# One factor chain at the beginning, squares on two engines, an own tile for an exp, side stages in more visits, rope tables kept: a hybrid mLSTM and sliding-window decoder layer

## The chip, the cores and the metric

The kernel runs on one core of one Trainium2 chip. Its time is the device time of one execution in microseconds. The profile is a trace of one execution; times inside it are counted from its first instruction. Engines are named as the profile names them: PE (matmuls; PEld for its weight loads), DVE (vector), ACT (scalar), POOL (GpSimd), SP (the queue that issues all DMAs here).

## The reference

One layer over a prompt of 1024 rows and 8 samples of 4 rows, width 1024, all in f32. Cut to what matters:

```python
mod = silu(c) @ w_ada + b_ada;  shift, scale, gate = split(mod, 3)
h = rmsnorm(x, g_norm) * (1 + scale) + shift
mq, mk, mv, mi, mf, mo, mz, aq, ak, av, az, gm, ga = split_in(h @ w_in)
# mLSTM branch: 4 heads of 128, scanned in chunks of 128 rows
b = cumsum(logsigmoid(mf + b_f)); d = b[t] - b[s] + (mi + b_i)[s], causal
m_hat = max(b + m, max(d)); s = (q k^T) * exp(d - m_hat)
num = s v + exp(b + m - m_hat) * (q C);  dot = sum(s) + exp(b + m - m_hat) * (q n)
y_m = norm(num / max(|dot|, exp(-m_hat))) * g_mn * sigmoid(mo) * silu(mz)
# attention branch: 8 heads of 64, 2 kv heads, window 128, a sink per head
q, k = partial_rope(aq), partial_rope(ak)
y_a = softmax_with_sink(q k^T / 8, window) v * silu(az)
u = sigmoid(gm) * (y_m @ w_mo) + sigmoid(ga) * (y_a @ w_ao)
y = rmsnorm(x + gate * (u @ w_o), g_final)      # plus new states and caches
```

The samples go through the same layer with states and caches of their own.

## The kernel before, in words

Products are in split f32: an operand is a high part and a rest, and three matmuls (high x high, high x rest, rest x high) stand for one product. `h` lies in SBUF transposed (features on partitions, the 1056 rows on the free axis), as eight blocks k of 128 features, in tiles `h_h` and `h_l`.

**Beginning.** `load_x` issues the loads of x in parts of 512 rows (p = 0 and 1, eight tiles each) and `xS` for the samples (p = 2). `x_sq` (from L337) squares the tiles on ACT, and PE sums them over partitions into `xs`, copied to `xsum`. `x_rs` turns the sums into columns (`xc`), computes one over the root with a chain of small DVE operations (`recip_sqrt`: `ssq`, `xr_y`, `xr_w`), and puts each block's factors on a diagonal (`xdg`). `x_rows` spreads them to rows with matmuls (`xb`), and `x_mul` multiplies x by them on DVE. `ada_chunk` makes 512 columns of the scale or the shift (`ada_sc`, `ada_sh`, transposed as `adat_sc`, `adat_sh`), which end in the tiles `A` and `B`. `h_part` then applies `A` and `B` on ACT and splits into `h_h` and `h_l`; `h_samples` does it for the samples. `pair` issues the first products (`g_ak`, `g_av`), first for the k of `half[0]`, then for those of `half[1]`. In the factor chains (L1471 to L1477) part 0 has a chain of its own and parts 1 and 2 share one. While `V.on` and `S.on` hold (to L1506), DVE and ACT keep the order in which the code issues.

**Main part.** Jobs of the product with `w_in` follow: four groups of queries (`queries`), then `mq`, `mk`, `mv` of four heads (`head_jobs`), then the gates as blocks of a Strassen-like scheme (`block_products`, `bx`, `by`, `bz`, `bw`), then `att_out`, `mem_out` and the product with `w_o` (`fo`). PE's order is written out when the program is built. Beside the main products, `Side` steps generators: a generator issues some operations and yields a lag and the PSUM pools that its next visit needs; `side.now` counts modelled product time, and a generator is visited again when its lag is over, its pools aren't used in the same tick, and 2.0 have passed since the last visit with products. The generators are:

- `gates` (L515): the sums of the mLSTM gates, in steps. The tile `bTs` is stored to `m_s` and then overwritten by its exp (L636), which is transposed a visit later (L648). A row of sums is copied from PSUM as `row`.
- `unit(g, b0)` (L740): 16 units of attention, two blocks of 128 queries each: scores `sc`, masked maximum on DVE (`mx`, `nmx`), exps on ACT (`p`, `den`), division on DVE, transposes `pt`, product `oT`. From `sc` to the division all is issued in one visit, and the transposes 11.0 later.
- `head(h)` (L941): three groups of chunks a head, in stages a (transposes `tk`, `tv`, the exps of `et` with a mask added by POOL), b (`S`, `U`, states `C`), c (`n`, sums of squares, `factors`: 13 or more small DVE operations) and d (transposes `ty`).
- `sample_head(h)` (L1051): the same for the samples; a step makes the tiles `vm` from `vf` on DVE and ACT, and products `sU` and `st` follow.
- `sum_blocks`: sums of blocks of `h` for the gates' scheme.

DVE, ACT, POOL and SP execute in the order that a scheduler lays down when the program is built, from priorities and modelled times; each is a queue, and an instruction that waits holds up all behind it. Most SBUF tiles come from a pool `half` of 42 buffers, raw weights from one of 9, and PSUM tiles from four pools (g, a, b, o) of two banks each. `rope_load` loads the cosine and sine tables: six tiles for the keys in `attention_begin`, and six again in each of the four `queries(g)`. `rope` uses them: a shuffle and two operations on DVE, one on POOL.

Of the kernel before, what the change touches and what calls it, by code (L numbers as in the profile page):

```python
# [26 lines left out]
NH = 4  # L27
# [131 lines left out]
def body(tc, a):  # L159
    nc = tc.nc  # L160
    with ExitStack() as ctx:
# [104 lines left out]

        xT = [load_x(p) for p in range(2)]
        xS = ht([128, KT, NS], "xS")
        dma(xS, a["xS"])
        xT.append([xS[:, k] for k in range(KT)])  # L270

# [65 lines left out]
        def x_sq(p):  # L337
            n = PARTS[p][1]
            acc = po([128, 512], f"xs{p}")
            if p == 2:  # L340
                sqs = ht([128, KT, NS], "xsq2")
                S.activation(sqs, xS, AF.Square)
            for k in range(KT):
                if p == 2:
                    sq = sqs[:, k]
                else:
                    sq = ht([128, 512], "xsq")
                    S.activation(sq, xT[p][k], AF.Square)
                j = 32 * (k % 4)
                mm(acc[j:j + 32, :n], one[:, 0:32], sq, start=(k < 4), stop=(k >= 4), share=4)  # L350
            sums = ht([128, 512], "xsum")
            S.copy(sums[:, :n], acc[:, :n])
            return sums

        def x_rs(ps_, sums):
            blocks = [(p, i, min(128, PARTS[p][1])) for p in ps_ for i in range(-(-PARTS[p][1] // 128))]
            nb = len(blocks)
            cols = pg([128, nb], f"xc{ps_[0]}")
            for j, (p, i, m) in enumerate(blocks):
                mm(cols[:m, j:j + 1], sums[p][:, i * 128:i * 128 + m], cst[:, C_S9:C_S9 + 1], start=True, stop=True)  # L360
            ssq = cp.tile([128, nb], F32, name=f"ssq{nb}")
            if m < 128:
                V.memset(ssq[:, nb - 1:nb], 1.0)
                V.tensor_scalar(ssq[:m, nb - 1:nb], cols[:m, nb - 1:nb], 1.0 / D, EPS, op0=ALU.mult, op1=ALU.add)
            full = nb - (m < 128)
            V.tensor_scalar(ssq[:, :full], cols[:, :full], 1.0 / D, EPS, op0=ALU.mult, op1=ALU.add)
            rs = recip_sqrt(ssq, [128, nb], f"xr{nb}")
            dgs = {p: ht([128, 512], f"xdg{p}") for p in ps_}
            for j, (p, i, m) in enumerate(blocks):
                V.tensor_scalar(dgs[p][:m, i * 128:i * 128 + m], ident[:m, :m], rs[:m, j:j + 1], None, op0=ALU.mult)  # L370
            return dgs
# [143 lines left out]
        def gates(zg, bias):  # L515
# [119 lines left out]
            dma(a["m_s"], v3(bTs)[:, :, 3])  # L635
            S.activation(bTs, bTs, AF.Exp, scale=-1.0)  # L636
            mle = cp.tile([NH, NS], F32, name="mle")
# [9 lines left out]
            fq = pb([128, 128], "fq2")  # L647
            tr(fq[:NS, 0:4], bTs, ident[:NH, :NH])  # L648
            tr(fq[:NS, 4:8], mle, ident[:NH, :NH])
# [44 lines left out]
        def ev_ak(p, acc, c0, n):  # L694
            k = ht([128, 384], "kr")[:, :n]
            S.copy(k, acc[:, :n])
            at["kl"] = ht([128, 384], "krr")
            t = rope(k, at["rope"][p], n, at["kl"], kD, c0)
            if p == 2:
                V.tensor_tensor(at["kTs"], k[:, 256:288], t[:, 256:288], op=ALU.add)  # L700
                del at["rope"]

# [37 lines left out]
        def unit(g, b0):  # L740
# [25 lines left out]
            v2 = lambda t: t.rearrange("p (k i) -> p k i", i=2)  # L766
            V.tensor_tensor(v2(nmx[:, 4:8]), sink[:, :, g:g + 1].to_broadcast((128, 2, 2)), v2(mx), op=ALU.subtract)
            den = sm([128, 4], "den", 3)
            S.activation(nmx[:, 4:8], nmx[:, 4:8], AF.Exp)
            for kv in range(2):  # L770
                for i, lo in enumerate(los):
                    j = 2 * kv + i
                    S.activation(p[kv][:, i, lo:], p[kv][:, i, lo:], AF.Exp, bias=nmx[:, j:j + 1],
                                 accum_out=den[:, j:j + 1])
            V.tensor_tensor(den, den, nmx[:, 4:8], op=ALU.add)
            V.reciprocal(den, den)
            for kv in range(2):
                for i, lo in enumerate(los):
                    j = 2 * kv + i
                    V.tensor_scalar(p[kv][:, i, lo:], p[kv][:, i, lo:], den[:, j:j + 1], None, op0=ALU.mult)  # L780
            yield 11.0, "b"
            pT = [ht([128, 4, 128], f"pT{kv}") for kv in range(2)]
# [21 lines left out]
        def queries(g):  # L804
            cs = [rope_load(p) for p in range(3)]

# [134 lines left out]
        def head(h):  # L941
# [11 lines left out]
            def stage_a(p):  # L953
# [22 lines left out]
                G.tensor_tensor(et[:, :m], et[:, :m], cmask.unsqueeze(1).to_broadcast((128, m, 128)), op=ALU.add)  # L976
                for i in range(m):
                    S.activation(et[:, i], et[:, i], AF.Exp, bias=an[:, j0 + i:j0 + i + 1])
                qw = ht([128, 3, 128], "qw")
                dma(qw[:, :m], st["wid"][j0:j0 + m].unsqueeze(0).to_broadcast((128, m, 128)))  # L980
                G.tensor_tensor(qw[:, :m], qw[:, :m], q[:, :w].rearrange("p (c e) -> p c e", e=128), op=ALU.mult)
                w_[p] = q, k, kn, vn, vw, et, qw, ns

            def stage_b(p):
# [21 lines left out]
            def stage_c(p):  # L1006
# [10 lines left out]
                for i in range(m):  # L1017
                    jk = sm([128, 128], "mjk", 2, BF16)
                    S.activation(jk, ns[:, i, 0:128], AF.Square, accum_out=ssq[:, i:i + 1])
                f = factors(ns[:, :m, 128], fl[:, j0:j0 + m], ssq[:, :m], [128, m], f"f{m}")  # L1020
                for i in range(m):
# [14 lines left out]

            for visit in ([(load, 0), 10.0, "b"], [(stage_a, 0), 13.0, "o"], [(stage_b, 0), (load, 1), 10.0, "ob"],
                          [(stage_c, 0), (stage_a, 1), 13.0, "o"], [(stage_b, 1), (load, 2), 4.0, "b"], [(stage_d, 0), 6.0, "ob"],
                          [(stage_c, 1), (stage_a, 2), 13.0, "o"], [(stage_b, 2), 4.0, "b"], [(stage_d, 1), 6.0, "o"],
                          [(stage_c, 2), 15.0, "b"], [(stage_d, 2), 0.0, ""]):  # L1040
                for fn, p in visit[:-2]:
# [9 lines left out]
        def sample_head(h):  # L1051
# [21 lines left out]
            S.activation(et, et, AF.Exp, bias=an[:NS, 32 + h:33 + h])  # L1073
            V.tensor_tensor(et, et, S_[:NS], op=ALU.mult)
            qd = ht([128, 8, 36], "qd")
# [7 lines left out]
            for b, m in zip(bs, ns_):  # L1083
                vf, vm = ht([NS, 512], f"vf{h}"), ht([96, 512], f"vm{h}", F32R)
                w = m * 129 + m % 2
                if m % 2:
                    G.memset(vf[:, w - 1:w], 0.0)
                V.tensor_tensor(vf[:, :m * 129].rearrange("p (b e) -> p b e", e=129), vn.unsqueeze(1).to_broadcast((NS, m, 129)),
                                wm[:, b].unsqueeze(2).to_broadcast((NS, m, 129)), op=ALU.mult)
                S.copy(vm[0:32, :w], vf[:, :w])  # L1090
                V.tensor_tensor(vm[32:64, :w], vf[:, :w], vm[0:32, :w].bitcast(F32), op=ALU.subtract)
                V.tensor_copy(vm[64:96, :w], vf[:, :w])
                vms.append(vm)
            yield 9.0, "o"
            num = po([128, 129], f"sn{h}")
# [8 lines left out]
            for i, (c, b, m) in enumerate(zip(Cs, bs, ns_)):  # L1104
                up = pb([128, 388], f"sU{h}_{i}")
                mm(up[:, :m * 129 + m % 2], kn, vms[i][:, :m * 129 + m % 2], start=True, stop=True)
                V.tensor_tensor(c[:, :m], c[:, :m], up[:, :m * 129].rearrange("p (b e) -> p b e", e=129), op=ALU.add)
# [8 lines left out]
            jk = sm([128, 128], "mjk", 2, BF16)  # L1116
            S.activation(jk[:NS], ns[:, 0:128], AF.Square, accum_out=ssq)
            f = factors(ns[:, 128:129], fls[:, h:h + 1], ssq, [NS, 1], "fs")
            V.tensor_scalar(ns[:, 0:128], ns[:, 0:128], f, None, op0=ALU.mult)
            yield 13.0, "b"  # L1120
            ty = pb([128, NS], f"sty{h}")
# [71 lines left out]
        def sum_blocks():  # L1193
            for n in ("t2", "t3", "t4"):
                blocks[n] = []
            for k in range(4):
# [4 lines left out]
                G.tensor_tensor(b22, b22, b12, op=ALU.subtract)  # L1201
                G.tensor_tensor(b11, b11, b22, op=ALU.add)
                yield 2.0, ""
                block_split("t3", k, b22)
                yield 1.0, ""
                block_split("t2", k, b11)
# [263 lines left out]
        sh1 = ada_chunk(ada_load(1, "sh1", "l1"), "sh1", shift_done(1))  # L1470
        sums = {0: x_sq(0)}  # L1471
        dgs = x_rs((0,), sums)
        sums[1] = x_sq(1)
        rows = {0: x_rows(0, dgs[0])}
        sums[2] = x_sq(2)
        x_mul(0, rows[0], half[0])
        dgs.update(x_rs((1, 2), sums))  # L1477
        steps(sc0, 3)
        for p in (1, 2):
            rows[p] = x_rows(p, dgs[p])  # L1480
        run(sc0)
        x_mul(1, rows[1], half[0])
        x_mul(2, rows[2], None)
        run(sh0)
# [4 lines left out]
        for k in half[0]:  # L1489
            h_part(k, 0)  # L1490
            if k == 0:
                prefetch(order[1])
        pair(half[0], 0, acc[0])
        for k in half[0]:
            h_part(k, 1)
        steps(sc1, 3)
        pair(half[0], 1, acc[1])
        h_samples(half[0])
        x_mul(0, rows[0], half[1])
        x_mul(1, rows[1], half[1])  # L1500
# [293 lines left out]
```

## Time and profile before

| | us |
|---|---|
| median of three runs | 906.91 |
| the three runs | 906.37, 906.91, 910.14 |
| the profiled execution | 909.59 |
| its span, first to last instruction | 907.8 |

Mean granted PE clock of the profiled execution: 0.977 of full speed. DMA: 118,380 packets, 152 MB, 167 GB/s on average, but 309 GB/s in the first 20 us and 400 in the next 20.

The page gives the busy time of each engine, and the span in 40 slices. The table of waits says which engine stood still before which instruction, and whose result ended the wait. The timeline lists instructions in order of time with the idle time before each. A view of stretches gives busy times and the granted clock between two moments. An engine's idle time costs only where PE in the end waits for it, since PE is the busiest.

### The profile page before, as it was taken

How to read it: one execution, taken by the hardware profiler on the slowest of the kernel's cores; microseconds unless marked ns; L12 is line 12 of the kernel's file. 1: busy time of each engine (PE TensorE's matmuls, PEld its weight loads, DVE VectorE, ACT ScalarE, POOL GpSimd, SP SyncE). 2: the span in 40 equal slices, each digit the busy share in tenths (PEclk: the TensorE clock that was granted, in tenths of full speed). 3: DMA queues.
4: the chain of work that ended last, by engine and by line, in shares of the span. 5: the costliest groups of instructions: out<-in, count | busy, mean ns of one | idle time of the engine just before them, and what ended most of it. 6: DMA issues, size and time to landing. Idle time of an engine off the chain costs nothing. (4 is left out here: it accounts for less than half of the span.)

```text
span 907.8 us, 15634 instructions
## 1 busy us (share of the span) xinstructions
PE 854.1 (94%) x5306; PEld 720.8 (79%) x5306; DVE 567.2 (62%) x1611; ACT 350.2 (39%) x892; POOL 228.3 (25%) x244
## 2 busy tenths in 40 slices
PE   7789969999999989889999999989999999999996
PEld 2478969888888979768888876757778899997775
DVE  3765655465676687683574346666765566747785
ACT  5542223433434435443545444434434432213231
POOL 0102211001032345643333222244534302220000
PEclk9799979999999999999999999999999999999998
DMA  8955665656565667525444333445322798543421
GB/s 321 392 197 196 207 187 175 206 175 202 169 157 135 194 181 207 150 80 176 127 124 127 107 112 108 139 127 170 115 86 78 251 337 286 176 133 111 151 76 48
DMA packets 118380, 151.98 MB, mean 167 GB/s; under 512 B 27516, under 2 KB 76028, under 8 KB 118268
## 3 DMA queue, kind: packets, MB, share of 16 engines
q1 hardware_dynamic: 118300, 150.98, 53.6%
q8 instruction: 42, 0.69, 0.3%
q14 instruction: 38, 0.31, 0.1%
HBM read 112.45 MB, written 39.51 MB: 167 GB/s over the span
## 5 line engine op out<-in xcount | busy, mean ns | idle before, releaser
L205 ACT ACTIVATE p<-p,nmx 128x256 f32<-128x256 f32 (+1 forms) x64 | 31.0, 487 | 39.8 <-DVE nmx L205 38.2
L227 PE MATMUL g_w_ao<-ya,wh_w_ao 128*128 128x384 f32 (+1 forms) x192 | 45.5, 322 | 0.9 <-ACT bw L205 0.5
L227 PE MATMUL g_w_mo<-ym_l,wh_w_mo 128*128 128x384 f32 (+1 forms) x192 | 45.7, 323 | 0.0
L972 POOL TENSOR_SCALAR hv<-vn,wend 128x129 f32<-128x129 f32 x32 | 20.4, 651 | 72.3 <-issue 29.4
L227 PE MATMUL g_mq<-h_h,wh_mq 128*128 128x384 f32 (+1 forms) x96 | 32.7, 341 | 3.5 <-ACT mk L205 3.5
L227 PEld LDWEIGHTS g_w_ao<-ya,wh_w_ao 128*128 128x128 f32 x192 | 33.4, 188 | 1.5 <-ACT bw L205 0.9
L227 PE MATMUL g_mv<-h_h,wh_mv 128*128 128x384 f32 (+1 forms) x96 | 32.8, 342 | 1.4 <-ACT mk L205 1.4
L227 PE MATMUL g_aq<-h_h,wh_aq 128*128 128x384 f32 (+1 forms) x96 | 33.4, 348 | 0.6 <-ACT zg L205 0.6
L227 PEld LDWEIGHTS g_w_mo<-ym_l,wh_w_mo 128*128 128x128 f32 x192 | 33.5, 188 | 0.0
L227 PE MATMUL g_mk<-h_h,wh_mk 128*128 128x384 f32 (+1 forms) x96 | 32.7, 341 | 0.0
L227 PE MATMUL g_aq<-h_l,wh_aq 128*128 128x384 f32 (+1 forms) x96 | 32.0, 333 | 0.0
L227 PE MATMUL g_aq<-h_h,wl_aq 128*128 128x384 f32 (+1 forms) x96 | 31.9, 333 | 0.0
L205 ACT ACTIVATE fjk<-rows_l 128x512 bf16<-128x512 f32 (+2 forms) x19 | 11.6, 610 | 51.2 <-issue 25.6
L227 PE MATMUL g_mq<-h_h,wl_mq 128*128 128x384 f32 (+1 forms) x96 | 31.1, 324 | 0.0
L227 PE MATMUL g_mq<-h_l,wh_mq 128*128 128x384 f32 (+1 forms) x96 | 31.0, 323 | 0.0
L227 PE MATMUL g_mk<-h_l,wh_mk 128*128 128x384 f32 (+1 forms) x96 | 31.0, 323 | 0.0
L227 PE MATMUL g_mv<-h_l,wh_mv 128*128 128x384 f32 (+1 forms) x96 | 31.0, 323 | 0.0
L227 PE MATMUL g_mk<-h_h,wl_mk 128*128 128x384 f32 (+1 forms) x96 | 31.0, 323 | 0.0
L227 PE MATMUL g_w_mo<-ym_l,wl_w_mo 128*128 128x384 f32 (+1 forms) x96 | 31.0, 323 | 0.0
L227 PE MATMUL g_mv<-h_h,wl_mv 128*128 128x384 f32 (+1 forms) x96 | 31.0, 323 | 0.0
L227 PE MATMUL g_w_ao<-ya,wl_w_ao 128*128 128x384 f32 (+1 forms) x96 | 30.8, 321 | 0.0
L205 DVE CUSTOM_DVE_ANT_0 p<-sc,cst,sink 128x256 f32<-128x256 f32 (+1 forms) x64 | 26.3, 462 | 6.7 <-PE sc L227 6.5
(1320 smaller groups left out, 2772.5 us busy)
## 6 DMA issues: line engine op xcount, KB each, us to landing
hb<-hD SPq DMA_DIRECT2D x24, 256.0 KB, 3.8
x<-xT SPq DMA_DIRECT2D x16, 256.0 KB, 5.2
early_h<-w_ada SPq DMA_DIRECT2D x8, 512.0 KB, 6.9
early_l<-w_ada SPq DMA_DIRECT2D x8, 512.0 KB, 10.5
hD<-x SPq DMA_DIRECT2D x16, 256.0 KB, 2.4
adar_ga<-w_ada SPq DMA_DIRECT2D x16, 256.0 KB, 5.4
wr_ga<-w SPq DMA_DIRECT2D x16, 256.0 KB, 2.9
wr_gm<-w SPq DMA_DIRECT2D x16, 256.0 KB, 3.1
```

Source lines behind the costliest of these rows:

```text
L205: ins = f(*args, **kw)
L227: in_order(nc.tensor.matmul(out, lhsT, rhs, start=start, stop=stop, skip_group_check=more))
L972: G.tensor_scalar(vw[:, i], vn[:, i], wend[:, j0 + i:j0 + i + 1], None, op0=ALU.mult)
```

## The change

It does the following.

- The loads: `xS` is issued ahead of x. The squares of odd k go to DVE. The sums of all three parts are made first, and one chain `x_rs((0, 1, 2))` follows; every second diagonal is written by ACT. The steps of `sh0` are issued ahead of the rest of `sc0`. `x_mul(2)` goes behind the first `h_part` loop, and `x_mul(0, rows[0], half[1])` ahead of the second.
- The exp of `bTs` goes to a tile of its own, `ebs`.
- `unit` gets two more visits, between the maximum and the exps, and between the exps and the division. In `head`, the exps of `et` become `stage_a2` and the factors `stage_c2`. In `sample_head`, the product with `S_`, ACT's copies and DVE's rests of `vm` get visits of their own, and so do the factors. The lags are divided. In `sum_blocks` the lags differ.
- `queries` uses the tables of `attention_begin`, which are no longer dropped.

```diff
-        xT = [load_x(p) for p in range(2)]
         xS = ht([128, KT, NS], "xS")
         dma(xS, a["xS"])
+        xT = [load_x(p) for p in range(2)]
...
-                    S.activation(sq, xT[p][k], AF.Square)
+                    if k % 2:
+                        V.tensor_tensor(sq, xT[p][k], xT[p][k], op=ALU.mult)
+                    else:
+                        S.activation(sq, xT[p][k], AF.Square)
...
-                V.tensor_scalar(dgs[p][:m, i * 128:i * 128 + m], ident[:m, :m], rs[:m, j:j + 1], None, op0=ALU.mult)
+                o = dgs[p][:m, i * 128:i * 128 + m]
+                if j % 2:
+                    S.activation(o, ident[:m, :m], AF.Copy, scale=rs[:m, j:j + 1])
+                else:
+                    V.tensor_scalar(o, ident[:m, :m], rs[:m, j:j + 1], None, op0=ALU.mult)
...
             dma(a["m_s"], v3(bTs)[:, :, 3])
-            S.activation(bTs, bTs, AF.Exp, scale=-1.0)
+            ebs = cp.tile([NH, NS], F32, name="ebs")
+            S.activation(ebs, bTs, AF.Exp, scale=-1.0)
...
-            tr(fq[:NS, 0:4], bTs, ident[:NH, :NH])
+            tr(fq[:NS, 0:4], ebs, ident[:NH, :NH])
...
             V.tensor_tensor(v2(nmx[:, 4:8]), sink[:, :, g:g + 1].to_broadcast((128, 2, 2)), v2(mx), op=ALU.subtract)
+            yield 2.5, ""
             den = sm([128, 4], "den", 3)
...
+            yield 3.0, ""
             V.tensor_tensor(den, den, nmx[:, 4:8], op=ALU.add)
...
-            yield 11.0, "b"
+            yield 5.0, "b"
...
-            cs = [rope_load(p) for p in range(3)]
+            cs = at["rope"]
...
-                for i in range(m):
-                    S.activation(et[:, i], et[:, i], AF.Exp, bias=an[:, j0 + i:j0 + i + 1])
...
+            def stage_a2(p):
+                j0 = h * 8 + GROUPS[p][0]
+                et = w_[p][5]
+                for i in range(len(GROUPS[p])):
+                    S.activation(et[:, i], et[:, i], AF.Exp, bias=an[:, j0 + i:j0 + i + 1])
...
+                w_[p] = ns, ssq
+
+            def stage_c2(p):
+                m, j0 = len(GROUPS[p]), h * 8 + GROUPS[p][0]
+                ns, ssq = w_[p]
                 f = factors(ns[:, :m, 128], fl[:, j0:j0 + m], ssq[:, :m], [128, m], f"f{m}")
...
-            for visit in ([(load, 0), 10.0, "b"], [(stage_a, 0), 13.0, "o"], [(stage_b, 0), (load, 1), 10.0, "ob"],
-                          [(stage_c, 0), (stage_a, 1), 13.0, "o"], [(stage_b, 1), (load, 2), 4.0, "b"], [(stage_d, 0), 6.0, "ob"],
...
+            for visit in ([(load, 0), 10.0, "b"], [(stage_a, 0), 7.0, ""], [(stage_a2, 0), 6.0, "o"],
+                          [(stage_b, 0), (load, 1), 10.0, "ob"], [(stage_c, 0), (stage_a, 1), 3.0, ""], [(stage_c2, 0), 4.0, ""],
+                          [(stage_a2, 1), 6.0, "o"], [(stage_b, 1), (load, 2), 4.0, "b"], [(stage_d, 0), 6.0, "ob"],
...
+                V.tensor_copy(vm[64:96, :w], vf[:, :w])
+                vms.append((vf, vm, w))
+            yield 4.0, ""
+            V.tensor_tensor(et, et, S_[:NS], op=ALU.mult)
+            for vf, vm, w in vms:
                 S.copy(vm[0:32, :w], vf[:, :w])
+            yield 2.5, ""
+            for vf, vm, w in vms:
                 V.tensor_tensor(vm[32:64, :w], vf[:, :w], vm[0:32, :w].bitcast(F32), op=ALU.subtract)
...
-            yield 9.0, "o"
+            yield 4.0, "o"
...
-        sums = {0: x_sq(0)}
-        dgs = x_rs((0,), sums)
-        sums[1] = x_sq(1)
-        rows = {0: x_rows(0, dgs[0])}
-        sums[2] = x_sq(2)
+        sums = {p: x_sq(p) for p in (2, 0, 1)}
+        dgs = x_rs((0, 1, 2), sums)
+        steps(sc0, 3)
+        rows = {p: x_rows(p, dgs[p]) for p in range(3)}
         x_mul(0, rows[0], half[0])
-        dgs.update(x_rs((1, 2), sums))
-        steps(sc0, 3)
-        for p in (1, 2):
-            rows[p] = x_rows(p, dgs[p])
+        steps(sh0, 3)
         run(sc0)
         x_mul(1, rows[1], half[0])
-        x_mul(2, rows[2], None)
         run(sh0)
...
+        x_mul(2, rows[2], None)
         pair(half[0], 0, acc[0])
+        x_mul(0, rows[0], half[1])
         for k in half[0]:
             h_part(k, 1)
...
         h_samples(half[0])
-        x_mul(0, rows[0], half[1])
         x_mul(1, rows[1], half[1])
```

More of the change, by code (lines that the diff above doesn't have):

```diff
@@ L700, in ev_ak @@
                 V.tensor_tensor(at["kTs"], k[:, 256:288], t[:, 256:288], op=ALU.add)
-                del at["rope"]
         def ev_av(p, acc, c0, n):
@@ L1035, in stage_d @@
                 dma(yhD[h][:, c0:c0 + w], y)
-            for visit in ([(load, 0), 10.0, "b"], [(stage_a, 0), 13.0, "o"], [(stage_b, 0), (load, 1), 10.0, "ob"],
-                          [(stage_c, 0), (stage_a, 1), 13.0, "o"], [(stage_b, 1), (load, 2), 4.0, "b"], [(stage_d, 0), 6.0, "ob"],
-                          [(stage_c, 1), (stage_a, 2), 13.0, "o"], [(stage_b, 2), 4.0, "b"], [(stage_d, 1), 6.0, "o"],
-                          [(stage_c, 2), 15.0, "b"], [(stage_d, 2), 0.0, ""]):
+            for visit in ([(load, 0), 10.0, "b"], [(stage_a, 0), 7.0, ""], [(stage_a2, 0), 6.0, "o"],
+                          [(stage_b, 0), (load, 1), 10.0, "ob"], [(stage_c, 0), (stage_a, 1), 3.0, ""], [(stage_c2, 0), 4.0, ""],
+                          [(stage_a2, 1), 6.0, "o"], [(stage_b, 1), (load, 2), 4.0, "b"], [(stage_d, 0), 6.0, "ob"],
+                          [(stage_c, 1), (stage_a, 2), 3.0, ""], [(stage_c2, 1), 4.0, ""], [(stage_a2, 2), 6.0, "o"],
+                          [(stage_b, 2), 4.0, "b"], [(stage_d, 1), 6.0, "o"], [(stage_c, 2), 3.0, ""], [(stage_c2, 2), 9.0, "b"],
+                          [(stage_d, 2), 0.0, ""]):
                 for fn, p in visit[:-2]:
@@ L1073, in sample_head @@
             S.activation(et, et, AF.Exp, bias=an[:NS, 32 + h:33 + h])
-            V.tensor_tensor(et, et, S_[:NS], op=ALU.mult)
             qd = ht([128, 8, 36], "qd")
@@ L1089, in sample_head @@
                                 wm[:, b].unsqueeze(2).to_broadcast((NS, m, 129)), op=ALU.mult)
+                V.tensor_copy(vm[64:96, :w], vf[:, :w])
[3 more added lines that the diff above has]
+            for vf, vm, w in vms:
                 S.copy(vm[0:32, :w], vf[:, :w])
+            yield 2.5, ""
+            for vf, vm, w in vms:
                 V.tensor_tensor(vm[32:64, :w], vf[:, :w], vm[0:32, :w].bitcast(F32), op=ALU.subtract)
-                V.tensor_copy(vm[64:96, :w], vf[:, :w])
-                vms.append(vm)
-            yield 9.0, "o"
+            yield 4.0, "o"
             num = po([128, 129], f"sn{h}")
@@ L1105, in sample_head @@
                 up = pb([128, 388], f"sU{h}_{i}")
-                mm(up[:, :m * 129 + m % 2], kn, vms[i][:, :m * 129 + m % 2], start=True, stop=True)
+                mm(up[:, :m * 129 + m % 2], kn, vms[i][1][:, :m * 129 + m % 2], start=True, stop=True)
                 V.tensor_tensor(c[:, :m], c[:, :m], up[:, :m * 129].rearrange("p (b e) -> p b e", e=129), op=ALU.add)
@@ L1117, in sample_head @@
             S.activation(jk[:NS], ns[:, 0:128], AF.Square, accum_out=ssq)
+            yield 2.5, ""
             f = factors(ns[:, 128:129], fls[:, h:h + 1], ssq, [NS, 1], "fs")
             V.tensor_scalar(ns[:, 0:128], ns[:, 0:128], f, None, op0=ALU.mult)
-            yield 13.0, "b"
+            yield 9.0, "b"
             ty = pb([128, NS], f"sty{h}")
@@ L1202, in sum_blocks @@
                 G.tensor_tensor(b11, b11, b22, op=ALU.add)
+                yield 4.0, ""
+                block_split("t3", k, b22)
                 yield 2.0, ""
-                block_split("t3", k, b22)
-                yield 1.0, ""
                 block_split("t2", k, b11)
```

## The prediction

> **What bounds the kernel now.** I read the page's busy table and clock row first, then PE's table of waits, and then the timeline at each long wait.
>
> ```profile
> PE 854.1 (94%) x5306; PEld 720.8 (79%) x5306; DVE 567.2 (62%) x1611; ACT 350.2 (39%) x892; POOL 228.3 (25%) x244
> ...
> PEclk9799979999999999999999999999999999999998
> ```
>
> PE is busy for 94% of the span and no matmul is removed, so only PE's idle time (907.8 - 854.1 = 53.7 us) and its half-clock stretches can go. PE's table of waits names them (waiter, releaser: us in total, times, longest):
>
> ```profile
> PE pt L232 <- DVE row L205: 7.2, 1, 7.2
> PE xs L227 <- ACT xsq L205: 5.8, 1, 5.8
> PE by L227 <- DVE gt L205: 4.4, 2, 3.1
> PE sU L227 <- DVE Cs L205: 3.8, 4, 2.0
> PE g_mq L227 <- ACT mk L205: 3.5, 1, 3.5
> PE g_ak L227 <- DVE h_h L205: 2.6, 1, 2.6
> PE g_av L227 <- DVE x L205: 2.3, 1, 2.3
> ...
> PE bx L227 <- DVE zt L205: 1.9, 1, 1.9
> ...
> PE g_mv L227 <- ACT mk L205: 1.4, 1, 1.4
> ```
>
> The longest one names DVE's `row`, but the timeline shows where it starts (start, us, engine, what, idle before and releaser; three answers, one for each engine):
>
> ```profile
> 127.96 0.23 ACT L205 ACTIVATE bTs<-bTs 4x32 f32<-4x32 f32 x1 [6.14 <-DMA m_s<-bTs]
> ```
> ```profile
> 128.73 0.69 DVE L205 TENSOR_TENSOR wl_mq<-wr_mq,wh_mq 128x512 fp32r<-128x512 f32 x1 [3.33 <-ACT wh_mq L205]
> ...
> 130.22 0.20 DVE L205 COPY row<-rp 1x64 f32<-1x64 f32 x1
> ```
> ```profile
> 130.48 0.90 PE L232 MATMUL pt<-cst,p 128*128 128x128 f32 x3 [7.18 <-DVE row L205]
> ```
>
> The exp of `bTs` writes in place over a tile that the store to `m_s` is still reading. ACT stands for 6.14 us; behind it queue `wh_mq` and the copy of `aq`, for which DVE's queue waits, and behind those stands `row`, whose PSUM bank PE needs for `pt`. The stretches (length, busy us of each engine, then the granted clock, DMA share and GB/s) show the second price:
>
> ```profile
> 126.18:136.42 10.24, 5.94 (x20) 5.94 (x21) 6.82 (x31) 2.92 (x10) 1.43 (x2) 0.50 0.69 190
> ...
> 334.39:337.80 3.41, 3.41 (x17) 3.18 (x17) 1.48 (x5) 0.07 (x1) 0.00 (x0) 0.50 0.81 231
> 406.33:409.48 3.15, 3.15 (x7) 2.48 (x8) 1.84 (x3) 2.24 (x4) 1.22 (x1) 0.50 0.36 142
> 593.80:597.22 3.42, 3.42 (x23) 1.86 (x22) 1.33 (x2) 0.61 (x2) 2.19 (x3) 0.50 0.52 174
> ```
>
> After each long wait PE works at half clock for a while: half of that work is lost time.
>
> **The change, part by part.** The sum is made on the profiled execution, 909.6 us.
>
> *Own tile for the exp (`ebs`).* The exp now reads `bTs` beside the store; its result is first read at 178.7. The wait costs 7.18 us idle, and 5.94 us of work at half clock add 5.94/2 = 2.97: 10.15. What is late next: in the changed program's order DVE must pass about 11 us of work between the unit's first `sc` and `row` (four custom ops 1.9, four p multiplications 1.0, three pieces of rope of about 1.6 each, two splits 1.4, small ops 2), and PE has 66 products of 0.13 to 0.175 us plus `sc`, `rp` and `pt`, about 15.5 us, in which DVE also waits some 2 us for ACT's exps. That is nearly even; I leave 1 us of the wait. Gain 9.1, bounds 5 and 10.2. On the clock, the Trainium skill (TensorE: Matmul & The Clock Gate, The HAM clock gate) says that full clock returns after about 3.4 us of sustained work. The row shows 5.94 us; by the rule the half-clock loss would be 1.7 and the sum 1.3 us smaller.
>
> *One factor chain at the beginning.* Now: square sums of part 0, its chain on DVE (14.54 to 17.8), multiplications, a second chain (22.27 to 25.9), `A`, four multiplications (2.47), `B` at 33.01, first product at 35.54. The DMA sets a floor: the x tiles land every 0.67 us, the last near 17 (its square starts at 16.9), and the shift weights follow the scale weights, four loads of 1.28 us each, done near 27. After: last square at 17.6, sums copied 18.8, nine `xc` 20.0, chain 2.6 (as 22.27 to 24.90 now) to 22.6, nine diagonals on two engines (0.22 each, five on DVE) to 23.8, `xb` to 25.4, `ada_sh` to 27.9, `adat_sc` 1.4, then `A`, the four multiplications of part 1 (2.5) and `B` at about 32.1. The split of the first weights on POOL (2.50 at 32.46) then runs before the first cast on DVE, which took 1.39 beside it and 0.42 without it. First product at about 33.5: gain 2.0, bounds 0 and 3.5. Eight of the sixteen squares go from ACT (0.63) to DVE; one a 0.67 us tile is hidden by the loads either way, and would cost 0.65 each if the loads were faster.
>
> *Multiplications of the second half moved ahead.* `g_av` waits 2.25 us at 47.45 because its PSUM bank holds the row factors, and `x_mul(0, half[1])` read them last, behind `h_samples`. It now stands ahead of `h_part(k, 1)`. DVE does 0.41 + 2.47 us more before part 1: its first h is then ready near 43.7 on the old time axis, PE comes there at 44.41, and the four k need 1.05 us of PE each against 0.9 of DVE, so nothing new waits. The wait goes, and with it most of the half clock from 47.67 to 51.08 (11 products at 0.32 instead of 0.175: 1.6). Gain 3.85, bounds 0 and 3.9.
>
> *Rope tables kept.* 24 table loads go from SP's queue and the DMA (192 or 144 KB each); DVE's wait of 5.4 us for `sin` before 117.6 goes; no PE wait hangs on it, and it gives the slack before `row` that the first part counts on. Six of 42 `half` buffers stay taken until the last query instead of being reloaded, so no more are held at a time. In the new order SP issues the `aq` weights of the next query behind the `kD` stores, which wait for DVE's rope, and ACT has `wh_aq` ahead of `vT` and `zg`: those loads take 4 us, so ACT may stand 0 to 1.5 us before a bank is free. I take 0.7 lost.
>
> *Side stages in more visits.* No operation is added. Three waits of PE come straight from an ACT or DVE queue that stands: 3.5 (`mk` behind unit exps, ACT idle 5.34 for `nmx` at 331.0), 1.4 (`mk` behind the exps of `et`, ACT idle 4.67 for POOL), 3.1 (`gt` behind the factor chain, at 406); the sample head's vm chain stands ahead of 1.3 and 1.9. Together 11.2, plus half of the three short half-clock stretches, (3.41 + 3.15 + 3.42)/2 = 5.0: 16.2. PE's order is fixed when the program is built, and it changes too: between a unit's `sc` and its `pt` lie on average 10.2 us of products instead of 10.0, but units (1, 2) and (3, 2) have 6.7 instead of 9.1, while the chain between them takes 1.9 (DVE) + 2.7 (ACT) + 1.6 (DVE) = 6.2 without queueing. Such new waits can't be read off the trace before: bounds are 16 gained and 10 lost (ten waits of 1 us, the size of the small ones in the table). I take half of 16, less 3 for these two units: gain 5.
>
> Sum: 9.1 + 2.0 + 3.85 - 0.7 + 5 = 19.25, so 890.3 on the profiled execution's axis. The median of the runs (906.9) lies 2.7 below that execution; where those 2.7 us come from isn't visible, so I carry half of them: 889.
>
> **The rivals.**
> *PE's fixed order becomes the bound (slower).* The visits put `pt`, `n`, `sU` at places chosen by modelled product time, and if the exps and factors now come later on ACT and DVE because other work was let ahead of them, PE stands at 16 units and 12 head groups. For: DVE is 62% busy, and factor ops of 0.16 us took 1.1 and 1.2 beside POOL (at 331.2 and 393.2). Against: the total lags are nearly the same. It decides from about 0.9 us a place: 28 x 0.9 = 25 cancels the 14.25 us of the other parts and the 11.2 of idle that goes. At 1.3 us a place: 28 x 1.3 = 36, 909.6 - 14.25 - 11.2 + 36 = 920, less 2.7: 917.
> *The gates' wait comes back under another name.* DVE's 11 us before `row` don't fit and 5 us of idle stay, the visits bring nothing, the start 4: 909.6 - 5.15 - 4 = 900, less 1.3: 899.
> *All of the visits' gain is kept:* 16.2 instead of 5, 878.
>
> **How the numbers follow.** Forecast 0.60, second rival 0.18, third 0.10, slower 0.12. About 0.5%, or 4.5 us, is what a measurement of this kernel can tell from no change (902.4 to 911.4). Of the second rival a third lies inside it (0.06), of the forecast's own tail 0.03, of the slower case 0.02: same 0.11, slower 0.10, faster 0.79. The range leaves out the slower case above 904 and the lowest part of the third rival: 877 to 904.
>
> **What would show it.** ACT's `ebs` without a wait for a DMA, no idle of PE over 2 us between 110 and 135, full clock there; the first `g_ak` at about 33.5 and no wait of `g_av` for x; waits of ACT for `nmx` (38.2 us now) and for POOL's `et` (29.1) cut by half or more. Wrong: `pt` waiting for DVE's p in many units, or a first product no earlier than 35.

## The result and the profile after

The changed kernel takes 895.9 us (median of four runs, 894.2 to 898.6); the kernel before takes 906.6. The ratio is 0.988 (95% interval 0.984 to 0.992): 1.2% faster, where 2.0% was forecast. The time lies in the range, on the forecast side, but only 10.7 of the 17.9 us came. The profiled execution of after took 898.62 us (span 896.8), 11.0 less than that of before.

PE's busy time and clock row on the page after:

```profile
PE 851.4 (95%) x5306; PEld 719.5 (80%) x5306; DVE 576.2 (64%) x1602; ACT 347.2 (39%) x888; POOL 230.7 (26%) x244
...
PEclk9899999999999989899999999999999999999999
```

PE's table of waits after (waiter, releaser: us in total, times, longest):

```profile
PE xs L227 <- ACT xsq L205: 7.0, 3, 4.8
PE g_ak L227 <- DVE h_h L205: 4.0, 1, 4.0
PE oT L227 <- DVE et L205: 3.5, 1, 3.5
PE n L227 <- DVE mx L205: 3.4, 1, 3.4
PE by L227 <- ACT by L205: 2.8, 1, 2.8
PE U L227 <- DVE uqv L205: 2.4, 1, 2.4
...
PE bw L227 <- ACT bw L205: 2.0, 1, 2.0
...
PE pt L232 <- DVE row L205: 1.1, 1, 1.1
```

The first two, in the beginning, have grown: `xs` from 5.8 to 7.0, `g_ak` for `h_h` from 2.6 to 4.0. Of the other old names `row` fell from 7.2 to 1.1, and `mk`, `gt`, `x` and `zt` are no longer in these lines. But five new waits stand in their place, 14.1 us together, all between 298 and 416. The stretches at half clock (length, busy us of each engine, granted clock, DMA share, GB/s) moved there as well:

```profile
329.59:336.41 6.82, 6.20 (x25) 6.21 (x26) 4.25 (x24) 3.82 (x17) 1.78 (x4) 0.50 0.44 168
360.31:363.72 3.41, 3.41 (x14) 3.41 (x12) 0.29 (x1) 0.58 (x1) 0.00 (x0) 0.50 0.39 116
377.37:380.79 3.42, 3.42 (x11) 2.65 (x9) 3.28 (x7) 0.00 (x0) 2.62 (x3) 0.50 0.00 0
414.92:418.33 3.41, 3.13 (x11) 2.85 (x12) 3.08 (x3) 1.83 (x6) 2.30 (x2) 0.50 0.33 85
```

I followed the same main products through both traces. The first product of `g_aq` starts at 77.49 before and at 72.77 after: 4.7 ahead. That of the second head's `mq` starts at 198.09 and 183.78: 14.3 ahead. The end is 11.0 ahead. So the beginning and the gates gained 14.3 together, and what follows lost 3.3 of it.

The timeline at the gates shows the first step as forecast: ACT's `ebs` has no wait ahead of it, and `pt` waits 1.12; the clock there is full (1.00 from 119 to 126).

```profile
108.61 0.21 ACT L205 ACTIVATE ebs<-bTs 4x32 f32<-4x32 f32 x1
```
```profile
119.69 0.55 PE L232 MATMUL pt<-cst,p 128*128 128x128 f32 x3 [1.12 <-DVE row L205]
```

### The profile page after: what moved, and what is told of

Read it like the earlier page. It is cut to its first block, busy times and chain, and to the rows that moved or that the text cites. A ratio compares the mean times of both kernels' runs of the same rounds, so it can differ in the third digit from the quotient of the medians.

```text
span 896.8 us, 15564 instructions
## 1 busy us (share of the span) xinstructions
PE 851.4 (95%) x5306; PEld 719.5 (80%) x5306; DVE 576.2 (64%) x1602; ACT 347.2 (39%) x888; POOL 230.7 (26%) x244
## 5 line engine op out<-in xcount | busy, mean ns | idle before, releaser
L205 ACT ACTIVATE p<-p,nmx 128x256 f32<-128x256 f32 (+1 forms) x64 | 30.9, 484 | 50.5 <-DVE nmx L205 45.6
L227 PEld LDWEIGHTS g_w_mo<-ym_l,wh_w_mo 128*128 128x128 f32 x192 | 33.5, 188 | 0.0
L227 PE MATMUL g_mv<-h_h,wh_mv 128*128 128x384 f32 (+1 forms) x96 | 33.5, 349 | 0.0
```

Of the source, the lines that this page charges most:

```text
L205: ins = f(*args, **kw)
L227: in_order(nc.tensor.matmul(out, lhsT, rhs, start=start, stop=stop, skip_group_check=more))
```

## The experiments

Two questions were open. Do the parts outside the side stages bring by themselves what the sum gave them? And why did what follows the gates lose 3.3 us, when I had put a gain of 5 for the visits? Times are medians; a ratio is to the kernel before in the same session, with its 95% interval. The experiments come from three sessions on three chips, so kernels of different sessions are best compared by their ratios.

**The own tile alone (e1).** In the kernel before:

```diff
-            S.activation(bTs, bTs, AF.Exp, scale=-1.0)
+            ebs = cp.tile([NH, NS], F32, name="ebs")
+            S.activation(ebs, bTs, AF.Exp, scale=-1.0)
...
-            tr(fq[:NS, 0:4], bTs, ident[:NH, :NH])
+            tr(fq[:NS, 0:4], ebs, ident[:NH, :NH])
```

> The kernel before with the own tile ebs alone. Theory: the wait of 7.2 us and the half-clock work behind it go almost whole; on PE's time axis the changed kernel was 4.7 us ahead at the first product of aq and 14.3 ahead at the one of the second head's mq, so 9.6 us belong here: 906.6 - 9.6 = 897.0 (896 to 898.5). Rival: this needs the rope tables to be kept too, because DVE's 5.4 us wait for sin stands ahead of row in this kernel: about 5 us of idle of PE stay ahead of pt, and the time is 901 to 903.

Measured: 905.4, ratio 0.998 (0.997 to 1.000). Neither theory: by the ratio the gain is 1.5 us (0 to 3), less than the rival gave. ACT's wait is gone, and PE still waits:

```profile
129.17 0.90 PE L232 MATMUL pt<-cst,p 128*128 128x128 f32 x3 [4.36 <-DVE row L205]
```

DVE is late at `row` by itself. Before it, it stood for a rope table and then for `m0`:

```profile
119.30 0.79 DVE L205 TENSOR_TENSOR ropet<-ropet,sin 128x384 f32<-128x384 f32 x1 [5.58 <-DMA sin<-rope]
...
122.42 0.18 DVE L205 TENSOR_TENSOR cms<-cms,m 4x32 f32<-4x32 f32 x1 [1.68 <-DMA m<-m0T]
```

**The own tile and the kept rope tables (e12).** The diff of e1, and:

```diff
-                del at["rope"]
...
-            cs = [rope_load(p) for p in range(3)]
+            cs = at["rope"]
```

> The kernel before with ebs and the kept rope tables, nothing else. Theory: with ebs alone pt still waited 4.4 us, since DVE had stood 5.6 us for sin and 1.7 for the load of m0 and was late at row by itself; with the tables kept the two together give what the changed kernel has at this place: wait of pt at most 2.5, 5 to 8 us faster than before (907.6): 900 to 902.5. Rival: the load of m0, not that of sin, makes DVE late; pt still waits 4 us and the time is that of ebs alone, 905.4 within 1.5.

Measured: 904.2, ratio 0.994 (0.991 to 0.997). In its trace DVE no longer waits for `sin` and `pt` waits 2.62 instead of 4.36. The median misses the expected 900 to 902.5 by 1.7 and lies within the rival's 1.5 of 905.4, but the rival's wait of 4 us for `pt` did not come. By ratios the two edits are worth 0.6% (5.5 us) where one was worth 0.2%, so the tables that I had booked as a loss of 0.7 bring about 4, give or take 3. PE's order is the same in both traces. The shorter wait for `pt` accounts for 1.7 of the 4; where the rest lies is not shown.

**The new beginning alone (e6).** In the kernel before, the hunks of `load_x`, `x_sq`, `x_rs` and the order of the beginning from the change.

> The kernel before with the new beginning alone (part of samples loaded first, squares on two engines, one factor chain, x_mul(0, half[1]) ahead of h_part(k, 1)). Theory: 5.1 us ahead at the gates' products as in the changed kernel, and the later wait for the store of m_s, of 7.2 us, moves along with it: 906.6 - 5.1 = 901.5 (900.5 to 903). Rival: the stretch of half clock that went with g_av's wait is not tied to that wait and turns up elsewhere, so that only 0.9 + 2.25 are left: 903.4.

Measured: 901.3, ratio 0.993 (0.991 to 0.996): the theory's time. The gain is 6.2 us, where the sum had 5.85 and the rival 3.15. But not all of it need be the beginning's: the theory had the wait of 7.2 us moving along unchanged, and in this trace `pt` waits 3.8. The first `g_aq` starts at 73.12 instead of 77.49, 4.4 ahead.

**No additional visits (e2).** The changed kernel with `unit`, `head`, `sample_head` and `sum_blocks` as before.

> The changed kernel with every side stage (unit, head, sample head, block sums) in as many visits as before; ebs, the beginning and the kept rope tables stay. Theory: the additional visits cost time; the changed kernel is 14.3 us ahead at 243 us of its trace and only 11.0 at its end, so without them 895.9 - 3.3 = 892.6 (891 to 894), and PE has no idle time over 2 us and no second stretch of half clock between 290 and 380. Rival: the waits in that stretch come from the earlier start of all that follows, not from the visits, which gain 5 us as I predicted: 899 to 901.

Measured: 896.9, ratio 0.989 (0.986 to 0.991), against 0.988 for the changed kernel. The theory's 892.6 is wrong, and so is the rival's 900: taken together the additional visits are worth nothing that can be measured. So the parts outside the visits gain 10.4 us (8 to 13), where the sum had 14.25 for them. In this trace, though, the waits are the old ones:

```profile
PE g_mq L227 <- ACT mk L205: 4.5, 1, 4.5
PE by L227 <- DVE gt L205: 4.2, 2, 2.9
...
PE pt L232 <- DVE row L205: 2.3, 1, 2.3
PE bx L227 <- DVE zt L205: 1.9, 1, 1.9
PE g_mv L227 <- ACT mk L205: 1.2, 1, 1.2
```

So the changed kernel, with its visits, has lost these waits and got others of the same sum: PE's idle time in the three stretches of the table below is 21.4 us here and 22.0 after. With the half-clock loss it is 25.8 and 30.1, and the two profiled executions, 894.2 and 898.6, lie as far apart.

**Sample heads and block sums in more visits, units and heads as before (e8).**

> The changed kernel with units and heads in as many visits as before; sample heads and block sums keep the additional ones. Theory: the loss lies with units and heads (new waits of 2.4 to 3.5 us at n, U and oT between 300 and 360), and the sample heads' visits gain (waits of 1.9 for bx and 2.0 for sU gone near 600): faster than without any additional visits by about 3: 888 to 891. Rival: the sample heads' waits go with any other order of the side work, and this kernel is within 1 us of the one without additional visits.

Measured: 887.8, ratio 0.978 (0.976 to 0.980): the fastest of all, 9 us under e2 and 8 under the changed kernel. That seemed to say where the good and the bad visits are. But the theory's path did not come with its time: `bx` still waits for `zt` here, 2.1 us where e2 has 1.9. The next runs tested this.

**Heads split, units not (e3), and units split, heads not (e4)**, both with sample heads and block sums split:

> The changed kernel with only the units' visits as before; heads, sample heads and block sums keep the additional ones. Theory: the heads' separate stages for the factor chain and the exps cost, because the factor chain on DVE then falls ahead of a unit's score operations (n waited 3.4 us for mx at 330): about as slow as the changed kernel, 894 to 897. Rival: the units cost, because a unit's exps and multiplications are queued behind other work when they come later (pT late, oT waiting 3.5 us at 359): 887 to 890 here, like the kernel with sample heads and block sums alone.

> The changed kernel with only the heads' visits as before; units, sample heads and block sums keep the additional ones. Theory (heads cost): 886 to 889, and no wait over 2 us between 290 and 420. Rival (units cost): 894 to 897.

Measured: e3 900.3, ratio 0.991 (0.987 to 0.994); e4 892.7, ratio 0.984 (0.980 to 0.988). By ratios, against e8, the heads' visits cost 11 us, the units' visits 5, and the two together 9. Neither expectation came as a whole: e3 is above both times, and e4 lies between them. 11 and 5 do not add up to 9, so there seems to be no price for each visit; the intervals are wide, though, and those of e4 and e8 just touch.

**Block sums alone (e10) and sample heads alone (e14).** The edit of the block sums is two lags:

```diff
                 G.tensor_tensor(b11, b11, b22, op=ALU.add)
-                yield 2.0, ""
+                yield 4.0, ""
                 block_split("t3", k, b22)
-                yield 1.0, ""
+                yield 2.0, ""
                 block_split("t2", k, b11)
```

> The changed kernel with units, heads and sample heads in as many visits as before; of the side stages only the block sums keep their change (the split of t3 is visited 4.0 instead of 2.0 after POOL's differences, that of t2 2.0 instead of 1.0 after it). Theory: the kernel with sample heads and block sums changed was 9.1 faster than the one with neither, and its trace differs from that one's most between 300 and 400 us, where the waits of mk for the unit's exps (4.5) and of by for gt (2.9) went; so at least 6 of the 9 belong to the block sums: 888 to 891. Rival: the 9 us belong to the sample heads, and this kernel takes the 896.9 of the one without additional visits, within 1.5.

> The changed kernel with units, heads and block sums in as many visits as before; only the sample heads keep the additional ones. Both together made 887.8, the block sums alone 901.5 and neither 896.9. Theory (sample heads' visits bring the gain, the block sums little): 886 to 890. Rival (neither change is worth anything by itself; each alters the places of all later stages in PE's order, and the time depends on how these places fall): anything from 889 to 901, and then most likely not near 888.

Measured: e10 901.5, ratio 0.992 (0.989 to 0.994); e14 901.8, ratio 0.994 (0.992 to 0.996). Against neither change (e2, 0.986 to 0.991) e14 is slower; the interval of e10 overlaps, so the block sums alone are at best no gain. Both together are 1.1% faster than neither. Both theories fall, and so does the rival of e10. The rival of e14 holds in kind; 901.8 lies 0.8 above its times.

PE's order can't carry the difference between e14 and e8. By the tiles of the traces, PE issues its 5306 matmuls in the same order in e8, e14 and e17 below (and in e2 and e10, but for one swap). Yet e14 takes 901.8 and e8 887.8, and e17, in the same session as e14, 889.3. The two lags act on the side work of POOL, ACT and DVE. In e14 ACT stands 5.16 us for a block sum of POOL, the copy `bw` stands behind that, and PE waits 5.4 us for the copy; in e8 PE has no such wait. ACT's timeline, then PE's waits, in e14:

```profile
378.55 0.62 ACT L205 CAST t4h<-hb 128x512 fp32r<-128x512 f32 x1 [5.16 <-POOL hb L1242]
379.07 0.58 ACT L205 COPY bw<-bx 128x512 f32<-128x512 f32 x1
```
```profile
PE bw L227 <- ACT bw L205: 5.4, 1, 5.4
```

**A figure without meaning (e15 in e8, e16 in e2).** The first lag of a unit, which is the time that its loads get:

```diff
-            yield 12.0, sc_bank[1]
+            yield 12.2, sc_bank[1]
```

> The kernel with sample heads and block sums in more visits (887.8), with one figure changed that has no meaning for any visit: the first lag of a unit is 12.2 instead of 12.0 us of products, so that most later stages stand at other places of PE's order. Theory (the places decide, not the visits): the time moves by 3 us or more, most likely up: 891 to 899. Rival (the visits of sample heads and block sums are worth 9 us wherever the stages stand): 886 to 890.

> The changed kernel with no additional visits (896.9), with the same figure changed: the first lag of a unit is 12.2 instead of 12.0. Theory (the places decide): it moves by 3 us or more, up or down. Rival: 895 to 898.5.

Measured: e15 896.3, ratio 0.988 (0.985 to 0.991), against 0.978 for e8 and 0.981 for e17, which has e8's order on PE and ran in the same session: the whole gain of these visits goes with a fifth of a microsecond in a lag. e16 900.7, ratio 0.993 (0.990 to 0.995), against 0.989: the same direction, but the intervals overlap, so this one is open. Part of what the fifth brought into e15 can be named. ACT stands ahead of the exps of `et`, `mk` stands behind them, and PE behind `mk`. ACT's timeline, then PE's waits:

```profile
363.80 0.98 ACT L205 ACTIVATE et<-et,an 128x128 f32<-128x128 f32 x3 [6.95 <-POOL et L983]
364.69 0.47 ACT L205 ACTIVATE mk<-g_mv 128x384 f32<-128x384 f32 x1
```
```profile
PE bx L227 <- ACT mk L205: 3.3, 1, 3.3
PE bw L227 <- ACT bw L205: 2.3, 2, 1.7
```

The stretch 290:380 of after, e8 and e15, in that order (columns as above):

```profile
290.00:380.00 90.00, 76.63 (x524) 70.32 (x523) 62.40 (x168) 36.00 (x104) 41.65 (x42) 0.93 0.50 148
```
```profile
290.00:380.00 90.00, 85.72 (x642) 78.29 (x641) 67.04 (x191) 39.24 (x112) 44.44 (x46) 1.00 0.62 184
```
```profile
290.00:380.00 90.00, 84.52 (x600) 77.71 (x601) 59.27 (x179) 38.74 (x111) 40.76 (x43) 0.98 0.67 182
```

Against e8, PE loses 1.2 us of busy time and 1.7 us by the clock in these 90 us in e15, and 9.1 and some 6 in the changed kernel. (The counts of matmuls differ by more, but the matmuls are not of one length, so a count says little.) By the table below, e15 also lost 3.4 us by the clock before 250.

**`m0` loaded early (e17).** In e8 the load of `m0` moves to the top of `gates`:

> The kernel with sample heads and block sums in more visits (887.8), with m0 loaded at the beginning of the gates' stage instead of right before it is used; the order on PE, ACT and DVE is the same. In the kernel without additional visits DVE stood 2.4 us for this load ahead of row, and PE then 2.3 us for row. Theory (the queue of DVE ahead of row sets what is left of pt's wait): the wait goes or falls below 0.7, and with it half-clock work if there is any: 885.5 (884 to 887). Rival (DVE makes the 2.4 us good before row, which stands behind the rope of the third piece and the unit's scores, and those wait for PE and POOL): pt still waits 2 us or more, 887 to 889.

Measured: 889.3, ratio 0.981 (0.978 to 0.983), no faster than e8. The rival holds, its time to 0.3: `pt` still waits 2.17, because `row` stands in DVE's queue behind the third piece's rope and the next unit's four score operations:

```profile
118.96 0.43 DVE L205 TENSOR_TENSOR aqr<-aq,ropet 128x256 f32<-128x256 f32 x1 [0.70 <-POOL aq L694]
...
119.69 0.48 DVE L205 CUSTOM_DVE_ANT_0 p<-sc,cst,sink 128x256 f32<-128x256 f32 x1
...
121.32 0.21 DVE L205 COPY row<-rp 1x64 f32<-1x64 f32 x1
```

**All traces in one account.** For three stretches I added PE's idle time and half of its busy time at half clock: from the first `g_aq` (its start in the first column) to 250, from 250 to 420, and from 420 to 720. One profiled execution each; the time of the same execution stands last.

| kernel | first `g_aq` | to 250 | 250 to 420 | 420 to 720 | its time |
|---|---|---|---|---|---|
| before | 77.5 | 8.4 + 3.0 | 11.3 + 3.3 | 8.3 + 1.7 | 909.6 |
| e1: own tile | 79.0 | 5.6 + 1.5 | 11.2 + 4.0 | 6.9 + 0 | 904.4 |
| e12: own tile, rope kept | 79.9 | 3.9 + 1.7 | 11.0 + 3.2 | 8.0 + 1.7 | 905.5 |
| e6: beginning | 73.1 | 5.9 + 1.5 | 13.0 + 4.4 | 7.1 + 0 | 901.5 |
| e2: all but the visits | 72.1 | 3.6 + 1.7 | 10.9 + 2.7 | 6.9 + 0 | 894.2 |
| after | 72.8 | 1.7 + 0 | 17.0 + 8.1 | 3.3 + 0 | 898.6 |
| e4: after, heads not split | 72.4 | 4.0 + 0 | 8.4 + 4.9 | 5.7 + 0 | 891.7 |
| e3: after, units not split | 72.6 | 4.4 + 1.6 | 16.1 + 7.0 | 2.9 + 0.9 | 901.5 |
| e8: after, neither split | 74.0 | 3.8 + 0 | 7.6 + 0 | 5.8 + 1.7 | 889.2 |
| e15: e8, lag 12.2 | 72.8 | 3.7 + 3.4 | 11.4 + 1.7 | 6.4 + 0 | 896.6 |
| e10: e2, block sums' lags | 72.9 | 3.9 + 1.7 | 14.4 + 4.5 | 7.2 + 0 | 901.2 |
| e14: e2, sample heads split | 73.3 | 4.3 + 1.7 | 15.2 + 4.1 | 6.5 + 0 | 901.7 |
| e16: e2, lag 12.2 | 72.7 | 3.4 + 1.7 | 14.0 + 1.7 | 7.0 + 0 | 896.8 |
| e17: e8, `m0` early | 73.6 | 3.4 + 1.7 | 5.7 + 1.7 | 5.8 + 1.7 | 889.5 |

A row's columns account for its time within about 1 us: after against before, 4.7 + (36.0 - 30.1) = 10.6, measured 11.0. e14 and e8 lie 12.5 apart, and 11.7 of this is lost between 250 and 420.

## Why the prediction was right, and too large

*Own tile.* The mechanism was right: the wait for the store went with it, and in the changed kernel 9.6 us were gained between the first `g_aq` and the second head's `mq`, where I had 9.1 - 0.7. But the term was put under the wrong name. `ebs` alone brought 1.5, and with the kept tables 5.5, where the two terms had 8.4: about 3 us of what is missing lie here. My step "That is nearly even; I leave 1 us of the wait" assumed a DVE that is not late. It is late as long as it waits for `sin` (e1), `pt` still waits 2.1 to 3.2 in the nine traces with the tables kept and the units in one visit, and only the two with the units in more visits have 1.1 (after) and 1.65 (e4). So the term looks like a joint one of three edits; the units' share rests on these two traces. Also, the 7.18 is not a fixed price: in e6 the same store held ACT up for 2.8 instead of 6.1, and `pt` waited 3.8.

*Rope tables.* Sign wrong: -0.7 forecast, about +4, give or take 3, by ratios (e12 against e1). I named the slack that they give and priced it at nothing of its own.

*The beginning.* Right in the main: 5.85 forecast, 6.2 measured by e6, where the first `g_aq` is 4.4 ahead. The first `g_aq` starts at 77.5, 79.0 and 79.9 in the three traces with the old beginning and at 72.1 to 74.0 in the eleven with the new one, 5.9 apart on average (4.7 between before and after). `g_av` no longer waits for x, and the half-clock stretch behind that wait is gone. The first product is the one sign that missed, at 34.62 instead of 33.5. The split of the weights on POOL, which I had moved away from the cast, now lies beside the second operation on `A`, which took 0.20 before. DVE's timeline, then POOL's:

```profile
29.48 1.29 DVE L205 TENSOR_TENSOR A<-A,vec 128x36 f32<-128x36 f32 x1
30.69 2.47 DVE L205 TENSOR_TENSOR x<-x,xb 128x512 f32<-128x512 f32 x4
33.08 0.18 DVE L205 TENSOR_TENSOR B<-adat_sh,vec 128x36 f32<-128x36 f32 x1
```
```profile
29.45 2.49 POOL L435 TENSOR_TENSOR wl_ak<-wr_ak,wh_ak 128x512 fp32r<-128x512 f32 x2 [28.39 <-ACT wh_ak L205]
```

The 0.20 us operation lasted until POOL's first one of about 1.25 ended. It lost 1.1 us, as much as lies between 33.5 and 34.6. The Trainium skill (SBUF — State Buffer, Who interferes with whom) says that a DVE instruction with two inputs in SBUF contends with a GpSimd instruction that reads SBUF, and that the pair of ports they share is an exclusive lock; this trace agrees, with 1.29 us for the operation that took 0.20.

*The visits.* This is the step that failed: "I take half of 16, less 3 for these two units: gain 5". They brought about 0 (e2 against after, 0.989 and 0.988), and that is the larger part of what is missing. In the changed trace the stretch from 250 to 420 has 25.1 us of idle and half-clock loss where before had 14.6, and the one from 420 to 720 has 3.3 where it had 10.0. So waits went and others came, and the two nearly cancel. The signs that I named as proof failed too. ACT's wait for `nmx` was to fall by half; it rose from 38.2 to 45.6, and that for POOL's `et` went only from 29.1 to 24.2:

```profile
ACT p L205 <- DVE nmx L205: 45.6, 12, 7.3
...
ACT et L205 <- POOL et L985: 24.2, 10, 6.9
```

That a visit or a lag has no price of its own is shown by e14, e8 and e15: what one change brings depends on the others. The change can act in two ways, by the places of the side stages in PE's order and by what then stands ahead of what in the queues of DVE, ACT and POOL. I had looked to PE's order. The second way alone is enough: e14 and e8 have one order on PE and lie 14 us apart. What PE's order adds was not separated; from e8 to e15 and e2 to e16 both change. Over the nine kernels that have the new beginning, the own tile and the kept tables and differ only in visits and lags (after, e2, e3, e4, e8, e10, e14, e15, e16), the ratio runs from 0.978 to 0.994. Removing waits "by name" and pricing them one by one was the wrong method here: the next order has other waits, here of about the same sum. The bounds for this term, +16 to -10, did hold what came; with a value of 0 the forecast would have been 894. The range of 877 to 904 was wide enough to hold a term that was 5 us off.

*The rivals.* The first one, PE's fixed order as the bound, was right in kind and not in size: PE stood where ACT and DVE had let other work ahead, at five places and not at 28, and it cost what the visits gained, not more. The second gave a time near the measured one by another way: the gates' wait did go.

How small work in these queues holds PE up can be read in e2, DVE's queue first, then POOL's:

```profile
314.53 1.06 DVE L205 TENSOR_SCALAR f2r_y<-f2v 128x2 int32<-128x2 int32 x1
...
317.97 0.99 DVE L205 TENSOR_TENSOR f2r_w<-f2r_w,f2v 128x2 f32<-128x2 f32 x1
...
319.29 1.01 DVE L205 SCALAR_TENSOR_TENSOR f2r_y<-f2r_w,f2r_y 128x2 f32<-128x2 f32 x1
```
```profile
314.27 1.29 POOL L1222 TENSOR_TENSOR hb<-hb,hb 128x512 f32<-128x512 f32 x1 [1.87 <-DMA hb<-hD]
317.65 1.29 POOL L1208 TENSOR_TENSOR hb<-hb,hb 128x512 f32<-128x512 f32 x1 [2.09 <-DMA hb<-hD]
319.02 1.26 POOL L1209 TENSOR_TENSOR hb<-hb,hb 128x512 f32<-128x512 f32 x1
```

Three operations of a head's factor chain, 0.16 us each elsewhere, end with POOL's block sums (315.59 and 315.56, 318.96 and 318.94, 320.30 and 320.28). They stand ahead of the unit's `nmx`, the exps stand behind that, `mk` behind the exps, and PE waits 4.46 for `mk`. In e8 the block sums and the chain fall differently, and this wait does not exist. That POOL's share in it is what separates e8 from e2 was not tested by itself.

## What to carry to other kernels

Where a program lays out the order of side work by lags, measure the spread of a lag that means nothing before you believe a 1% effect of one that does: here a change of 12.0 to 12.2 was worth nearly as much (0.7 to 1.0%) as the whole reorganisation (1.2%), though in a second kernel it was not clear of noise. Compare the orders themselves too: two versions with one order on PE lay 14 us apart, so the queues of the other engines have to be read as well. Edits that take a wait away for every order (a tile of its own for an in-place write, a table kept instead of reloaded, a chain shortened at the start) held up better: the new beginning was 5.9 us ahead on average whatever followed, and the wait for the store never came back. When a wait is removed, look at each queue between its releaser and the waiter for a second cause before booking the whole wait, because an instruction in an in-order queue has all earlier waits of that queue ahead of it; and of the versions that were run the one to keep is e8, at 0.978, as a good draw (e17, which has the same order on PE, gave 0.981).

## What the runs showed of the hardware

*The granted clock falls after shorter waits than I had thought, and by chance.* All half-clock stretches in the 14 traces between 60 and 850 us, where PE had been busy, last 3.41 us or two or three times that. Of PE's idle times from 0.9 to 1.85 us there, 1 of 64 came with one; from 1.85 to 2.5 us 11 of 24; from 2.5 to 2.95 us 6 of 9; from 2.95 us on all 22. The same wait of 1.87 to 1.88 for `zt` near 585 us came with one in before and e12 and with none in e1, e2, e6, e10 and e16. Two stretches, at 76 us in e15 and e16, had no such idle time ahead of them: PE's longest there was 0.61. Why they came is not shown; e2 and e8 have the same products there and no stretch. The Trainium skill (TensorE: Matmul & The Clock Gate, The HAM clock gate) describes a window of 3.4 us that runs free of the kernel, and the multiples and the chance agree with that; its table puts the fall after at least one idle window of about 3.4 us, and as a threshold for idle time that is too high here. Each half-clock window costs up to 1.7 us, half of 3.41. Runs of one kernel lie 3 to 13 us apart (e8 886.2 to 889.4, before 902.5 to 915.4 in one session). Part of this goes with the clock: the fastest of these runs of before has a mean granted clock of 0.982 and the slowest 0.972, which I estimate at up to 9 of the 13 us.

*The latency of one small store varied by a factor of two.* From the end of the write of `bTs` to the exp that waited for the store of it, 7.1 us passed in before and 3.7 in e6, with the same instructions around it; what made the difference is not shown.
